# A list-scheduled hybrid decoder trunk: new transfer costs in its planner, one strip for the compressed bias, and its gates computed with Tanh

## The chip, the cores and the metric

The kernel runs on one core of a Trainium2 chip. Its time is the device time of one execution in microseconds (us), as the median of the runs. The core has a matmul engine (TensorE, PE; its weight loads are shown as PEld), three engines for elementwise work (VectorE, DVE; ScalarE, ACT; GpSimd, POOL) and SyncE, whose queue (SP) issues every transfer of this kernel. Each engine is given its own list of instructions, and waits by semaphore for what another engine or a transfer has to deliver.

## The reference

Two layers on 1024 tokens of width 1024, in float32. Each layer is `x + rms_post(W_out[(A | B | C) * silu(z)])` with `h = rms_pre(x)`, and one projection of `h` gives the columns of all groups and the gate path `z`.

- A (4 heads of 64): the sum of three attentions, each times a sigmoid gate per token and head. The first sees compressed keys: 63 overlapping blocks of 32 tokens pass a two-layer network, `silu(blk @ w1) @ w2`. The second sees all earlier tokens (16 of 16 blocks are selected), the third the last 512.
- B (4 heads): latent attention; queries and keys come out of normed low-rank latents, with a rotary part.
- C (8 heads): a window of 128 tokens, with a learned sink per head.

A and C add a relative-position bias from a table of 32 buckets per head. What the change touches is

```python
p_c = softmax(where(valid_c, lc + bias[:, t5_bucket(pos - cend)], NEG)) * valid_c
g = sigmoid(gates)
mixed = concat([o_a, o_b, o_c]) * silu(z)
```

## The kernel before

**Number format and tiles.** Each f32 operand is split into two f16 halves, and a product is three f16 matmuls (high-high, high-low, low-high), scaled by powers of two (`SW` = 256 on weights, `SQ` = 16 on activations, `SM` = 16 on the mixed output). `split` is one ACT copy, which writes the high half, and one DVE op, which writes the remainder. Tokens go in 8 tiles of 128. The kernel uses 8 banks of PSUM: three for scores (psS), two for transposes (psT), one for attention outputs (psO), two for projections (psJ).

**Stages of a layer.** `first` projects values, keys and the compressed blocks. `second` is a generator of further projections (latents, queries); `run` lays its pieces between the units of the sliding-window attention C. `gate_path` is the next generator: 26 tiles (3 column groups of 8 token tiles, and 2 tiles of the fourth) of 24 matmuls each give `z` in 128x256 blocks, laid between the units of attention A. Each block is copied out of PSUM by ACT (line 864), and each pair of blocks is stored to device memory (line 866). `last_phase` runs the latent attention B, the last 6 gate blocks, the product with `W_out` and the residual; in layer 1 the pre-norm of layer 2 as well.

**A unit** of attention is one token tile and one or two heads, in three parts that `run` keeps some units apart: `score` (matmuls into psS, then per piece one DVE op that scales, adds the bias strip, stores to SBUF and keeps the running minimum, then one Exp on ACT with the row sum), `turn` (transposes and splits the probabilities; by transposing DMA from a staging buffer in the larger units of attentions A and C and in the latent attention of layer 2 from its third token tile on, by PE otherwise) and `values` (matmuls into psO). In the latent attention the last of four units ends with `end_mla`: DVE multiplies the four heads out of psO into columns 256 to 511 of the gate tile.

**The gate in the last phase.** For each token tile `gate` (line 1176) fetches 128x1024 of `z` into a tile `sz` (two buffers), applies SiLU on ACT over the full width (line 1179), and POOL multiplies in the outputs of A and C. After `end_mla`, `mixed` (line 1184) splits the whole tile and transposes it by DMA for the product with `W_out`. The table that ACT needs for SiLU, sigmoid or Exp is loaded by an instruction of its own wherever the function changes to one that the loaded table lacks.

**The compressed bias.** It depends on the token and the block's end, so on 16 times the block index less the token: within a row group a shift by 8 columns per token tile. For each token tile `score` fetched it with 8 small transfers (lines 900 to 905) from `bias_rows` in device memory into a tile for four heads, with two buffers; column 63 was set to the masking value once a layer (line 1112).

**The order.** Nothing is emitted as it is written. Every instruction is recorded as a `Step`, with the steps it depends on and the buffers it uses. `schedule` (line 273) then simulates the engines: each free engine takes, of its steps whose inputs and buffers are ready, the one with the smallest key. The key is the number in program order, and for transfers the negative length of the longest chain behind the step. Buffers of a tag are handed out in program order. The prices are in `cost` (line 244): for a transfer the issue time on SP, its share of one common bus, and a fixed time to landing. The order that comes out is the order of every engine's instructions.

Of the kernel before, what the change touches and what calls it, by code (L numbers as in the profile page):

```python
# [15 lines left out]
F32 = mybir.dt.float32  # L16
# [9 lines left out]
SW = 256.0  # L26
# [13 lines left out]
L_M = 126  # L40
# [48 lines left out]
def row_mask():  # L89
    return (np.arange(128) >= 31).astype(np.float32).reshape(128, 1)  # L90

# [55 lines left out]

class Room:
# [17 lines left out]
class Step:  # L166


    def __init__(self, n, engine, name, args, kwargs):
        self.n, self.engine, self.name, self.args, self.kwargs = n, engine, name, args, kwargs  # L170
        self.before, self.after, self.rooms, self.key = set(), [], [], n


class Recorder:
# [9 lines left out]
    def __init__(self, nc):  # L184
        self.nc, self.steps, self.rooms, self.seen, self.inner = nc, [], [], {}, set()
        for name in ("tensor", "vector", "scalar", "gpsimd", "sync"):
            setattr(self, name, Recorder.Engine(self, name))
# [15 lines left out]
    def add(self, engine, op, args, kwargs):  # L203
        s = Step(len(self.steps), engine, op, args, kwargs)
# [39 lines left out]
    def cost(self, s):  # L244
# [13 lines left out]
        if s.engine == "vector":  # L258
            t = 152.0 + 1.045 * n
# [9 lines left out]
        if s.name == "dma_start_transpose":  # L269
            return 1300.0, (400.0 + size / 220.0, 2000.0)  # L270
        return 520.0, (size / 200.0, 1900.0)

    def schedule(self, slots):
# [13 lines left out]
        for s in reversed(self.steps):  # L287
# [3 lines left out]
            s.key = -tail[s] if s.engine == "sync" else s.n  # L291
        events, order, bus, table, now = [], [], [0.0], [None], 0.0
# [25 lines left out]
        while True:  # L318
            for e, heap in ready.items():
                if heap and free[e] <= now:  # L320
# [4 lines left out]
                    if e == "scalar" and s.args[2] not in (AF.Copy, AF.Square, table[0]):  # L325
                        table[0] = s.args[2]
                        busy, seen = busy + 1283.0, seen + 1283.0
                    if e == "sync":
                        bus[0] = max(bus[0], now + busy) + seen[0]
                        seen = bus[0] + seen[1] - now  # L330
                    s.seen = now + seen
# [32 lines left out]
def trunk(ctx, tc, a, out):  # L364
# [67 lines left out]

    rows_d = nc.dram_tensor("bias_rows", (12, L_ALL), F32, kind="Internal").ap()
# [62 lines left out]
    def bias_setup():  # L496
# [4 lines left out]
        for c0 in range(0, L_ALL, 1024):  # L501
# [9 lines left out]
            dma(rows_d[:, c0:c0 + n], rw[:, :n])  # L511
        for h in range(4):
# [129 lines left out]
    def compress_hidden(L, l, xs):  # L642
# [5 lines left out]
        for s in range(2):  # L648
# [8 lines left out]
            nc.scalar.activation(hid[:, s, :NC_CMP], p[:, :NC_CMP], AF.Silu, bias=hb[:, s:s + 1], scale=1.0 / (SW * SQ))  # L657

    def compressed(L):
# [7 lines left out]
        split(p[:, :64], SQ, L.KM[:, 0], L.KM[:, 1])  # L667
        for half in range(2):
            nc.tensor.matmul(p[64 * half:64 * half + 64, 128:192], hid[:, 1], w2[:, 128:], start=True, stop=True)
        for half in range(2):  # L670
            r = slice(64 * half, 64 * half + 64)
            split(p[r, 128:192], SQ, L.VM[r, half, 0], L.VM[r, half, 1])

    def first(L, l, wv):
# [27 lines left out]
        nc.scalar.activation(L.G, L.G, AF.Sigmoid, scale=1.0 / SW)  # L702
# [156 lines left out]
    def gate_columns(L, w, g, t, zs):  # L859
# [4 lines left out]
        nc.scalar.activation(zt[:, t % 2], p[:, :256], AF.Copy, scale=1.0 / SW)  # L864
# [16 lines left out]
    class Unit:  # L881
# [9 lines left out]
        def score(u):  # L891
# [7 lines left out]
            if kind == "cmp":  # L899
                if "cm" not in g["tile"]:  # L900
                    cm = g["tile"]["cm"] = view(L.r, 3072 + 256 * (qt % 2), [128, 4, 64], F32)
                    for i in range(8):
                        dma(cm[i * 16:(i + 1) * 16, :, :NC_CMP],
                            rows_ap(0, O_M + 63 - 8 * qt - i, [[L_M, 16], [L_ALL, 4], [1, NC_CMP]]))
                cm = g["tile"]["cm"]
                b = u.b = u.rings[0].take([128, 128], F32)
                p = ps("S")
                for j in range(2):
                    h = u.h + j
                    r = slice(j * 64, j * 64 + 64)  # L910
                    for s in range(2):
                        nc.tensor.matmul(p[:, r], L.QA[:, h, qs], L.KM[:, s], start=(s == 0), stop=(s == 1))
                    ttr(b[:, r], p[:, r], cm[:, h], ALPHA, BIGF, mx[:, 3 * j:3 * j + 1])
# [3 lines left out]
            if kind == "swa":  # L917
# [4 lines left out]
                for j in range(2):  # L922
# [3 lines left out]
                    for s in range(2):  # L926
                        nc.tensor.matmul(p[:, r], L.QC[:, h, qs], L.KC[:, s, k0 * 128:k0 * 128 + nk],
                                         start=(s == 0), stop=(s == 1))
                    ttr(b[:, r], p[:, r], L.stC[:, h, 256 - nk:], ALPHA, L.nsink[:, h:h + 1], mx[:, col:col + 1])
# [123 lines left out]
    def run(units, filler, total, lag_t, lag_v):  # L1053
# [5 lines left out]
        for i in range(n + lag_v):  # L1059
# [7 lines left out]
            while more and spent < total * done / whole:  # L1067
                w = next(filler, None)
                more = w is not None
                spent += w or 0  # L1070
        for _ in filler:
            pass

# [15 lines left out]
    def nsa_units(L):  # L1089
# [8 lines left out]
        for qt in range(NT):  # L1098
            tile = {}
# [245 lines left out]
```

## Time and profile before

| | us |
|---|---|
| median of 3 runs | 1091.31 (1089.62 to 1092.93) |
| profiled execution, its time | 1093.32 |
| profiled execution, span of its instructions | 1091.5 |
| PE busy / weight loads | 998.0 / 669.3 |
| DVE busy | 760.5 |
| ACT busy | 691.0 |
| POOL busy | 117.2 |

The mean granted PE clock is 0.968 of full speed. How to read it: a group line names the engine, the operation, what it writes and reads, shapes, the count, then busy time and the mean of one, then the idle time of the engine just before, with what ended it. Nearly all instructions bear line 359, where the planned order is emitted, so groups are told apart by their tiles. A stage begins and ends in the order of the plan, not at a barrier, so the windows by which the span is cut are cut by eye: the sliding-window stage of layer 1 from 115 to 233 us, attention A from 233 to 404, the latent stage from 404 to 558; in layer 2 from 640, 751 and 923.

### The profile page before, as it was taken

The page shows a single profiled execution, that of the slowest core. Times are in us where ns is not written, and L with a number is a line of the kernel's source. Part 1 is how long each engine was busy: PE and PEld are TensorE (multiplying, and loading weights), DVE is VectorE, ACT ScalarE, POOL GpSimd, SP SyncE. Part 2 cuts the span into 40 slices and gives each one's busy share as a digit, 9 for nine tenths or more (in the row PEclk, how much of TensorE's full clock was granted, in tenths as well). Part 3 has the DMA queues.
Part 4 walks back from the last instruction along what each step waited for, and adds up shares of the span by engine and source line. Part 5 has one row for each costly group of instructions (what it writes and reads, how often), then busy time and mean ns, then how long its engine had stood idle before and what let it go on. Part 6 is the DMA issues. An engine that isn't in the chain of part 4 may idle for free. (4 is left out here: it accounts for less than half of the span.)

```text
span 1091.5 us, 25293 instructions
## 1 busy us (share of the span) xinstructions
PE 998.0 (91%) x9536; PEld 669.3 (61%) x9536; DVE 760.5 (70%) x2268; ACT 691.0 (63%) x1655; POOL 117.2 (11%) x198
## 2 busy tenths in 40 slices
PE   5998999989999988999999999998999999599975
PEld 2853657648887774565575465764887777245432
DVE  4744678847788967878765367884778897677742
ACT  5642667737777867778545267773787787867731
POOL 1000101001110112212000010100111011212100
PEclk9999999989999998999999999998999999699988
DMA  7586467675499995775575546867448999676982
GB/s 254 147 268 174 91 151 143 135 159 138 96 153 190 190 249 149 177 159 135 114 190 184 136 102 141 150 132 160 131 104 149 187 192 236 141 172 151 212 174 77
DMA packets 313498, 174.41 MB, mean 160 GB/s; under 512 B 273580, under 2 KB 289324, under 8 KB 313376
## 3 DMA queue, kind: packets, MB, share of 16 engines
q1 hardware_dynamic: 313376, 172.81, 69.9%
q8 instruction: 74, 1.21, 0.5%
q14 instruction: 48, 0.39, 0.1%
HBM read 76.63 MB, written 21.41 MB: 90 GB/s over the span
## 5 line engine op out<-in xcount | busy, mean ns | idle before, releaser
L359 PEld LDWEIGHTS <-HT 128*128 128x128 f16 x3084 | 252.1, 99 | 44.0 <-issue 11.0
L359 ACT ACTIVATE arena<-arena,mx 128x256 f32<-128x256 f32 (+8 forms) x384 | 226.8, 591 | 82.4 <-DVE mx L359 80.7
L359 PE MATMUL psJ<-W,HT 128*128 128x256 f16 (+1 forms) x2304 | 270.9, 264 | 2.0 <-ACT sz L359 1.8
L359 PEld LDWEIGHTS <-arena 128*128 128x128 f16 x3540 | 169.2, 99 | 80.8 <-issue 11.1
L359 PE MATMUL psJ<-HT,W 128*128 128x512 f16 x864 | 199.9, 388 | 9.5 <-DVE tmp L359 6.2
L359 PEld LDWEIGHTS <-W 128*128 128x128 f16 x864 | 85.1, 100 | 109.5 <-issue 16.5
L359 PE MATMUL psO<-V,arena 128*128 128x64 f16 x2304 | 103.2, 193 | 6.7 <-DMA arena<-sz 5.3
L359 DVE CUSTOM_DVE_ANT_0 arena<-psS,R 128x64 f32<-128x64 f32 (+4 forms) x192 | 86.9, 464 | 31.0 <-PE psS L359 23.7
L359 ACT ACTIVATE sz<-psJ 128x256 f32<-128x256 f32 (+1 forms) x92 | 40.4, 440 | 83.0 <-PE psJ L359 55.9
L359 POOL TENSOR_TENSOR rs<-rs,halfneg 128x1 f32<-128x1 f32 x64 | 35.0, 548 | 529.1 <-DVE rs L359 513.5
L359 PE MATMUL psS<-KA,QA 128*128 128x512 f16 (+3 forms) x384 | 82.5, 313 | 0.1
L359 DVE CUSTOM_DVE_ANT_0 arena<-psS,arena,nsink 128x256 f32<-128x256 f32 (+1 forms) x128 | 57.6, 461 | 27.8 <-PE psS L359 27.5
L359 PE MATMUL psS<-KB,QB 96*128 96x512 f16 (+3 forms) x288 | 64.2, 346 | 12.3 <-DVE mx L359 11.9
L359 ACT ACTIVATION_READ_ACCUMULATOR arena<-arena,mx 128x1 f32 x384 | 72.7, 189 | 0.0
L359 ACT ACTIVATE arena<-psT 128x128 f16<-128x128 f32 (+3 forms) x144 | 53.9, 383 | 25.4 <-PE psT L359 20.6
L359 DVE SCALAR_TENSOR_TENSOR arena<-psT,arena 128x128 f16<-128x128 f32 (+3 forms) x144 | 60.3, 430 | 11.8 <-ACT arena L359 11.3
L359 PEld LDWEIGHTS <-V 128*128 128x128 f16 x384 | 36.6, 100 | 51.0 <-DMA V<-ringS 10.0
L359 PE MATMUL psT<-ident,arena 128*128 128x128 f32 x300 | 59.5, 290 | 7.1 <-DVE arena L359 3.9
L359 DVE SCALAR_TENSOR_TENSOR W<-ringS,W 128x1024 f16<-128x1024 f32 x48 | 58.4, 1223 | 10.5 <-ACT W L359 10.3
L359 DVE SCALAR_TENSOR_TENSOR sz<-arena,sz 128x512 f16<-128x512 f32 (+4 forms) x76 | 57.6, 758 | 11.1 <-ACT sz L359 11.1
L359 PE MATMUL psJ<-R,arena 128*128 128x65 f16 (+1 forms) x384 | 55.2, 300 | 2.4 <-DMA arena<-ringS 2.4
L359 ACT ACTIVATE psJ<-psJ 128x512 f32<-128x512 f32 x32 | 18.6, 582 | 59.4 <-DVE tmp L359 59.4
(132 smaller groups left out, 1548.4 us busy)
## 6 DMA issues: line engine op xcount, KB each, us to landing
ringS<-in_w_in_dram SPq DMA_DIRECT2D x40, 512.0 KB, 4.6
gate_rows<-sz SPq DMA_DIRECT2D x32, 256.0 KB, 3.2
ringS<-in_w_out_dram SPq DMA_DIRECT2D x16, 512.0 KB, 6.6
sz<-gate_rows SPq DMA_DIRECT2D x16, 512.0 KB, 4.5
R<-in_x_dram SPq DMA_DIRECT2D x8, 512.0 KB, 4.8
ringS<-in_cmp_w_dram SPq DMA_DIRECT2D x8, 512.0 KB, 5.9
x<-in_rope_dram SPq DMA_DIRECT2D x8, 512.0 KB, 4.8
x<-in_x_dram SPq DMA_DIRECT2D x8, 512.0 KB, 4.2
```

Of the source, the lines that this page charges most:

```text
L359: getattr(getattr(self.nc, s.engine), s.name)(*[real(v) for v in s.args], **{k: real(v) for k, v in s.kwargs.items()})
```

## The change

- **Planner.** Prices for transfers and for short DVE operations are new: issue 400, 485 or 650 ns by kind, bus at 300 rather than 200 bytes per ns, landing 1300 (transposes 1100) plus `SLACK` of 1200 ns. A transfer is issued in the plan only when the eighth last one has landed. Steps that `run` takes from a generator (the filler) get 60 added to their key. Exp and Tanh count as one table.
- **Order of recording.** In units of two heads (compressed and sliding window) the matmuls of both heads are recorded ahead of the first head's DVE and ACT steps.
- **Compressed bias.** A resident tile `mstrip` of 128 x 4 x 120 is filled by 8 transfers after the bias rows are stored; each token tile takes a window of 64 columns of it. The rows in device memory are one column longer, which holds the mask. The 64 small transfers and two memsets of each layer go.
- **Gates.** SiLU and sigmoid become Tanh: `silu(u) = u * (1 + tanh(u/2)) / 2`. For `z` the Tanh is taken where the block leaves PSUM, a DVE operation multiplies by the value in PSUM, and twice the SiLU is stored; the factor goes into the scale of `mixed`'s split. The full-width SiLU of the last phase goes. The hidden layer of the compressed blocks and the gates of A are turned likewise, with small DVE operations.

```diff
-L_M = 126
+L_M = 127
+W_M = 120
...
+
+
+LATE = 60
+
+
+
+SLACK = 1200.0
...
+TABLE = {AF.Exp: 0, AF.Tanh: 0, AF.Silu: 1, AF.Sigmoid: 2}
...
-        self.before, self.after, self.rooms, self.key = set(), [], [], n
+        self.before, self.after, self.rooms, self.key = set(), [], [], n + late
...
-            t = 152.0 + 1.045 * n
+            t = max(152.0 + 1.045 * n, 250.0)
...
         if s.name == "dma_start_transpose":
-            return 1300.0, (400.0 + size / 220.0, 2000.0)
-        return 520.0, (size / 200.0, 1900.0)
+            return 900.0 + size / 600.0, (size / 300.0, 1100.0 + SLACK)
+        inner = isinstance(out, View) and isinstance(src, View)
+        return 400.0 if size > 500000 else 650.0 if inner else 485.0, (100.0 + size / 300.0, 1300.0 + SLACK)
...
-            s.key = -tail[s] if s.engine == "sync" else s.n
-        events, order, bus, table, now = [], [], [0.0], [None], 0.0
+            if s.engine == "sync":
+                s.key = -tail[s]
+        events, order, bus, table, lanes, now = [], [], [0.0], [None], [], 0.0
...
-                if heap and free[e] <= now:
+                if heap and free[e] <= now and (e != "sync" or len(lanes) < 8 or lanes[-8] <= now):
...
-                    if e == "scalar" and s.args[2] not in (AF.Copy, AF.Square, table[0]):
-                        table[0] = s.args[2]
+                    if e == "scalar" and TABLE.get(s.args[2], table[0]) != table[0]:
+                        table[0] = TABLE[s.args[2]]
                         busy, seen = busy + 1283.0, seen + 1283.0
...
+                        lanes.append(now + seen)
...
+        for i in range(8):
+            dma(mstrip[i * 16:(i + 1) * 16], rows_ap(0, O_M + 7 - i, [[L_M, 16], [L_ALL, 4], [1, W_M]]))
...
-            nc.scalar.activation(hid[:, s, :NC_CMP], p[:, :NC_CMP], AF.Silu, bias=hb[:, s:s + 1], scale=1.0 / (SW * SQ))
+            hv = sb([128, 2, 64], F32, "hv", 2)
+            nc.vector.tensor_scalar(hv[:, 0, :NC_CMP], p[:, :NC_CMP], 1.0 / (SW * SQ), hb[:, s:s + 1], op0=OP.mult, op1=OP.add)
+            nc.scalar.activation(hv[:, 1, :NC_CMP], hv[:, 0, :NC_CMP], AF.Tanh, scale=0.5)
+            nc.vector.scalar_tensor_tensor(hid[:, s, :NC_CMP], hv[:, 1, :NC_CMP], 1.0, hv[:, 0, :NC_CMP],
+                                           op0=OP.add, op1=OP.mult)
...
-        split(p[:, :64], SQ, L.KM[:, 0], L.KM[:, 1])
+        split(p[:, :64], SQ / 2, L.KM[:, 0], L.KM[:, 1])
...
-            split(p[r, 128:192], SQ, L.VM[r, half, 0], L.VM[r, half, 1])
+            split(p[r, 128:192], SQ / 2, L.VM[r, half, 0], L.VM[r, half, 1])
...
-        nc.scalar.activation(L.G, L.G, AF.Sigmoid, scale=1.0 / SW)
+        nc.scalar.activation(L.G, L.G, AF.Tanh, scale=0.5 / SW)
+        nc.vector.tensor_scalar(L.G, L.G, 0.5, 0.5, op0=OP.mult, op1=OP.add)
...
-        nc.scalar.activation(zt[:, t % 2], p[:, :256], AF.Copy, scale=1.0 / SW)
+        nc.scalar.activation(zt[:, t % 2], p[:, :256], AF.Tanh, scale=0.5 / SW)
+        nc.vector.scalar_tensor_tensor(zt[:, t % 2], zt[:, t % 2], 1.0, p[:, :256], op0=OP.add, op1=OP.mult)
...
             if kind == "cmp":
-                if "cm" not in g["tile"]:
-                    cm = g["tile"]["cm"] = view(L.r, 3072 + 256 * (qt % 2), [128, 4, 64], F32)
-                    for i in range(8):
-                        dma(cm[i * 16:(i + 1) * 16, :, :NC_CMP],
-                            rows_ap(0, O_M + 63 - 8 * qt - i, [[L_M, 16], [L_ALL, 4], [1, NC_CMP]]))
-                cm = g["tile"]["cm"]
+                cm = mstrip[:, :, 56 - 8 * qt:120 - 8 * qt]
...
                     for s in range(2):
                         nc.tensor.matmul(p[:, r], L.QA[:, h, qs], L.KM[:, s], start=(s == 0), stop=(s == 1))
+                for j in range(2):
+                    h = u.h + j
+                    r = slice(j * 64, j * 64 + 64)
                     ttr(b[:, r], p[:, r], cm[:, h], ALPHA, BIGF, mx[:, 3 * j:3 * j + 1])
                     expo(b[:, r], mx[:, 3 * j:3 * j + 1], sm[:, 3 * j:3 * j + 1])
...
                         nc.tensor.matmul(p[:, r], L.QC[:, h, qs], L.KC[:, s, k0 * 128:k0 * 128 + nk],
                                          start=(s == 0), stop=(s == 1))
+                for j in range(2):
+                    h = u.h + j
+                    col = h % 4
+                    r = slice(j * nk, j * nk + nk)
                     ttr(b[:, r], p[:, r], L.stC[:, h, 256 - nk:], ALPHA, L.nsink[:, h:h + 1], mx[:, col:col + 1])
                     expo(b[:, r], mx[:, col:col + 1], sm[:, col:col + 1])
...
             while more and spent < total * done / whole:
+                nc.late = LATE
                 w = next(filler, None)
+                nc.late = 0
                 more = w is not None
                 spent += w or 0
+        nc.late = LATE
         for _ in filler:
             pass
+        nc.late = 0
...
-        for i in range(2):
-            nc.vector.memset(view(L.r, 3072 + 256 * i, [128, 4, 64], F32)[:, :, 63:], MASKED)
...
         def gate(qt):
             sz = tiles[qt]["sz"] = sb([128, D], F32, "sz", 2)
             dma(sz, z_d[qt * 128:(qt + 1) * 128, :])
-            nc.scalar.activation(sz, sz, AF.Silu)
...
             hl = nxt["hl", 0]
-            split(g["sz"], SM, hl[:, 0], hl[:, 1])
+            split(g["sz"], SM / (2 * SW), hl[:, 0], hl[:, 1])
```

More of the change, by code (lines that the diff above doesn't have):

```diff
@@ L166, with __init__ @@
 class Step:
-    def __init__(self, n, engine, name, args, kwargs):
+    def __init__(self, n, late, engine, name, args, kwargs):
         self.n, self.engine, self.name, self.args, self.kwargs = n, engine, name, args, kwargs
-        self.before, self.after, self.rooms, self.key = set(), [], [], n
+        self.before, self.after, self.rooms, self.key = set(), [], [], n + late
 class Recorder:
@@ L185, in __init__ @@
         self.nc, self.steps, self.rooms, self.seen, self.inner = nc, [], [], {}, set()
+        self.late = 0
         for name in ("tensor", "vector", "scalar", "gpsimd", "sync"):
@@ L203, in add @@
     def add(self, engine, op, args, kwargs):
-        s = Step(len(self.steps), engine, op, args, kwargs)
+        s = Step(len(self.steps), self.late, engine, op, args, kwargs)
         self.steps.append(s)
@@ L431, in trunk @@
     nc.vector.memset(zero, 0.0)
+    mstrip = sb([128, 4, W_M], F32, "mstrip")
     rows_d = nc.dram_tensor("bias_rows", (12, L_ALL), F32, kind="Internal").ap()
@@ L1098, in nsa_units @@
         for qt in range(NT):
-            tile = {}
             for h in (0, 2):
-                g = {"tile": tile}
+                g = {}
                 r.append(Unit(L, "cmp", qt, h, g, None, rings))
```

## The prediction

> **What bounds the kernel now.** I read the page's busy shares first, then the span cut by stage, then who TensorE (PE) waited for, and last the timeline of the worst stretch.
>
> ```profile
> PE 998.0 (91%) x9536; PEld 669.3 (61%) x9536; DVE 760.5 (70%) x2268; ACT 691.0 (63%) x1655; POOL 117.2 (11%) x198
> ```
>
> PE is busy for 91% of the span, so no edit to another engine is worth more than the 93 us in which PE stands still, plus what PE loses while its granted clock is low. The stage table says where these are. Its columns are the window and its length, the busy time (and instructions) of each engine, the granted PE clock, the DMA share and GB/s.
>
> ```profile
> 0.00:26.00 26.00, 12.87 (x32) 5.46 (x33) 11.19 (x22) 12.79 (x21) 2.90 (x10) 1.00 0.73 260
> 26.00:115.00 89.00, 84.67 (x589) 51.03 (x589) 45.69 (x85) 37.91 (x71) 2.19 (x4) 0.98 0.64 183
> ...
> 233.00:404.00 171.00, 166.87 (x2053) 133.47 (x2053) 131.12 (x445) 124.27 (x331) 22.25 (x45) 0.98 0.80 162
> 404.00:558.00 154.00, 142.49 (x1099) 80.88 (x1095) 115.45 (x297) 106.39 (x188) 25.22 (x33) 0.94 0.64 158
> ...
> 751.00:923.00 172.00, 166.58 (x2057) 133.92 (x2056) 131.53 (x444) 123.85 (x333) 22.24 (x45) 0.98 0.80 159
> 923.00:958.00 35.00, 22.33 (x137) 10.95 (x138) 22.39 (x73) 26.69 (x45) 6.90 (x9) 0.71 0.64 174
> 958.00:1042.00 84.00, 80.25 (x628) 41.28 (x627) 61.72 (x167) 57.61 (x89) 15.28 (x15) 1.00 0.80 179
> 1042.00:1091.50 49.50, 29.92 (x196) 14.08 (x193) 14.94 (x22) 8.45 (x16) 1.64 (x3) 0.84 0.53 123
> ```
>
> The sparse attention stages (233 to 404, 751 to 923) leave PE only 4.1 and 5.4 us idle. The weak places are the latent attention stage of layer 1 (11.5 us idle, clock 0.94), the first 35 us of the same stage in layer 2 (12.7 us idle, clock 0.71) and the last 49.5 us (19.6 us idle, clock 0.84). The start idles 13.1 us before any of the changed work. In 923 to 958 PE waited for these, as total, times, longest:
>
> ```profile
> PE psS L359 <- DVE mx L359: 6.4, 3, 3.8
> PE psO L359 <- DVE sz L359: 3.9, 2, 3.0
> ```
>
> The timeline of ACT, DVE, SyncE's queue (SP) and PE shows what stands behind the 3.0 us: start, length, instruction.
>
> ```profile
> 940.04 1.04 ACT L359 ACTIVATE W<-ringS 128x1024 f16<-128x1024 f32 x1
> 941.09 1.28 ACT L359 ACT_TABLE_LOAD   x1
> 942.39 1.06 ACT L359 ACTIVATE sz<-sz 128x1024 f32<-128x1024 f32 x1
> ...
> 944.29 1.28 ACT L359 ACT_TABLE_LOAD   x1
> ...
> 943.48 0.86 DVE L359 SCALAR_TENSOR_TENSOR sz<-psO,rc,sz 128x64 f32<-128x64 f32 x4 [1.14 <-ACT sz L359]
> ...
> 936.62 0.33 SPq L359 DMA_DIRECT2D sz<-gate_rows  x1
> ...
> 944.39 1.12 PE L359 MATMUL psO<-VB,HT 128*128 128x64 f16 x18 [3.00 <-DVE sz L359]
> 947.64 0.58 PE L359 MATMUL psS<-KB,QB 96*128 96x512 f16 x1 [2.13 <-DVE mx L359]
> ```
>
> The gate tile is fetched at 936.62. ACT then loads a table (1.28) and applies SiLU (1.06); only now may DVE multiply the attention output by it, and only then is PE's one output bank free.
>
> **The change, part by part.** These groups give the prices: busy us, mean ns.
>
> ```profile
> L359 ACT ACT_TABLE_LOAD x35 | 44.9, 1283 | 3.0 <-DVE mx L359 1.7 <-PEq L1335 0.7
> L359 ACT ACTIVATE sz<-sz 128x1024 f32<-128x1024 f32 x16 | 16.9, 1056 | 0.9 <-DMA sz<-gate_rows 0.8
> L359 ACT ACTIVATE sz<-psJ 128x256 f32<-128x256 f32 x64 | 23.8, 374 | 29.4 <-PE psJ L359 18.8 <-DMA gate_rows<-sz 6.1 <-issue 2.9
> L359 DVE SCALAR_TENSOR_TENSOR W<-ringS,W 128x1024 f16<-128x1024 f32 x48 | 58.4, 1223 | 10.5 <-ACT W L359 10.3
> L359 DVE TENSOR_TENSOR QC<-psO,rc 128x256 f32<-128x256 f32 x32 | 13.4, 420 | 3.7 <-PE psO L359 2.9 <-DVE mx L359 0.2
> L359 ACT ACTIVATE arena<-arena,mx 128x256 f32<-128x256 f32 x136 | 68.4, 503 | 29.7 <-DVE mx L359 29.1
> ```
>
> *Tanh for SiLU and sigmoid.* If Tanh is served by the table that Exp uses, 34 of the 35 loads go: 34 x 1.283 = 43.6 us of ACT. The 16 full-width SiLUs go too: 16.9 us. All 16 and 28 of the loads lie in the latent stages, so ACT loses 52.8 us of its work there. The 64 copies of gate columns become 64 Tanh; no row has a Tanh, so it is bounded by the copy (0.374) and by an Exp of that width (0.503). I take the copy, since it too reads PSUM and has no bias or sum: no change, at worst 64 x 0.13 = 8.3 us of ACT.
>
> What of it reaches PE? Not the whole: in 958 to 1042 ACT made ten loads and five SiLUs, and PE was still busy 80.25 of 84 us. I count where PE stands. In 923 to 958 the waits on sz (3.9) go. The 2.13 us wait that ends at 947.64 and the 3.8 us one before it have a share of ACT's queue in them; the splits of the output weights keep their 1.2 us each on DVE, so I take half of 6.4, 3.2. The clock of 0.71 over 35 us is 10.2 us of lost cycles, of which half, 5, returns when the gaps that precede it go. Together 12. In 404 to 558 the clock lost 0.06 x 154 = 9.2 and idle is 11.5; less of it names the gate:
>
> ```profile
> PE psT L359 <- DVE arena L359: 2.4, 3, 1.4
> PE psS L359 <- DVE mx L359: 2.3, 3, 0.8
> PE psO L359 <- DVE sz L359: 0.5, 1, 0.5
> ```
>
> I take half of 2.4 + 2.3 + 0.5 and 3.4 of clock, 6. In the last 49.5 us one wait on sz goes, the 1.8 that the 3.9 and 0.5 leave of the 6.2 in the whole span (its row stands with the schedule, below): 2. **Sum -20.** The bounds: 0 (ACT never set PE's pace) and -45 (12.7 + 10.2 + 11.5 + 9.2 and 1.8, all idle and clock loss of the two stretches).
>
> The Trainium skill, ScalarE: Activation LUTs, "What ACT_TABLE_LOAD costs", prices a switch at 1283 ns of load plus a drain of about 1380 ns. The load agrees with the row to the nanosecond. The drain does not show: at 941.09 the load starts 0.01 us after the split before it. By the page ACT would be freed of 34 x 2.66 = 90 us, an estimate; the sum goes by the row.
>
> *The gate product on DVE.* Each of the 64 gate tiles gets a 128x256 scalar_tensor_tensor out of PSUM. The nearest row is 0.420 with f32 out of PSUM: 26.9 us of DVE, of which 26 tiles per layer, 10.9 us, lie in the sparse stage, where DVE then has 142 of 171 us. The projection bank (psJ, two of them) is now given back after ACT and DVE, not after ACT. PE works behind it on attention and on the other bank, which is the cover; without it every tile costs 0.42. Bounds 0 and +26.9; near the first, because that stage's PE has under 6 us idle and DVE 29 us free: **+3.** On SP, the store of the gate pair waits for that product too, and what is queued behind it is transposes.
>
> *Small ones.* Four hidden tiles get one tensor_scalar and one scalar_tensor_tensor of 63 columns, the gates one tensor_scalar per layer; four memsets go. At the 0.42 us of the 256-column row as a ceiling the ten are 4.2 us of DVE, in stages where it is half idle (45.69 of 89 us busy from 26 to 115): 0, bounds 0 and +4.2.
>
> *The bias strip.* One resident strip replaces 128 small transfers:
>
> ```profile
> L359 SPq DMA_DIRECT2D R<-bias_rows x128: 302/424/1766, 229.9 to 864.1; - x128
> ...
>   DVE arena L359: 3.1, 2
> ```
>
> (min/median/max ns on the queue; who waited for the landing, us, times.) SP is freed of 128 x 0.424 = 54 us of issue, and DVE of waits of 3.1 us. Eight issues of the same kind, 3.4 us, come into the bias setup behind the four row stores and ahead of the twelve replicating transfers. Bounds -3.1 and +3.4; the replicated rows are first read in the next stage, and DVE has slack where it waited: **-1.**
>
> *The schedule.* The planner's prices, the late fillers and two heads' scores issued ahead of their evictions change the order on every engine. By its own formula a 512 KB load was planned at 520 + 2621 + 1900 = 5.0 us and is now 400 + 100 + 1748 + 2500 = 4.7; a 128 KB copy inside SBUF goes from 3.1 to 3.7; a transpose of 128x1024 f16 from 4.9 to 4.5. Measured landings:
>
> ```profile
> ringS<-in_w_in_dram SPq DMA_DIRECT2D x40, 512.0 KB, 4.6
> ...
> QC<-sz SPq DMA_DIRECT2D x16, 128.0 KB, 3.0
> ...
> arena<-sz SPq DMA_TRANSPOSE x76, 3.7
> ```
>
> The plan was not far off before, so I expect a small gain from waits on landings. PE's waits on those are the prize, and the two stage borders the risk:
>
> ```profile
> PE psJ L359 <- DMA V<-ringS: 8.9, 3, 5.0
> PE psJ L359 <- DVE tmp L359: 6.2, 2, 3.2
> PE psO L359 <- DVE sz L359: 6.2, 4, 3.0
> PE psO L359 <- DMA arena<-sz: 5.3, 5, 1.9
> PE psO L359 <- DMA HT<-HT: 3.4, 1, 3.4
> PE psJ L359 <- DMA arena<-ringS: 2.4, 2, 2.1
> ```
>
> The DMA rows sum to 20.0 us. I take a quarter, **-5**; bounds -20 and, since a new order can as well create such waits, +13 (the 6.2 us of waits on DVE tmp at the borders and the clock loss of those stages, 2 x 0.02 x 171 = 6.8, once more).
>
> The sum is -20 + 3 + 0 - 1 - 5 = -23. The profiled execution took 1093.3 us (span 1091.5 and 1.8 around it), 2.0 above the median of 1091.3; against itself it goes to 1070.3, and the median to **1068**.
>
> **The rivals.** *DVE and the banks become the bound (slower).* Evidence for: DVE is at 77% in the sparse stages and would be at 83%, with W splits of 1.2 us in its queue ahead of a product that holds a bank. Against: two banks, and 24 matmuls per tile between two uses. It decides if a bank is held longer than PE has other work ready. Then all 26.9 us count, half of the 20 is eaten as the last gate tiles drain into the latent stage, and order gives 3: 1091.3 + 26.9 - 10 - 3 = 1105.
>
> *ACT's relief does not reach PE.* For: the 958 to 1042 row. Against: the 941 chain. Then the first term is 3, and 1091.3 - 3 + 3 - 1 - 2 = 1088.
>
> *The stalls and the low clock go entirely.* For: a low clock follows the gaps, so both go together. Against: the W splits at the stage's start. 12.7 + 10.2 of layer 2, 14 of layer 1's stage (two thirds of 11.5 + 9.2) and 10 (half of the waits on landings): 1091.3 - 47 = 1044.
>
> *Late fillers pile up at the stage ends.* Fillers now yield by 60 steps, so more projection is left when the attention units are out. The border shows the price of projections alone:
>
> ```profile
> 233.41 1.01 PE L359 MATMUL psJ<-HT,W 128*128 128x512 f16 x2 [3.16 <-DVE tmp L359]
> ```
>
> 3.2 us and 3.4 of clock (0.02 x 171), in each layer: as much again is +13, so 1068 + 13 = 1081.
>
> *The loads stay.* Were Tanh not in Exp's table, every gate tile in the sparse stage would cost two loads: 52 x 2.57 = 133 us of ACT, 124 + 67 = 191 us in a stage of 171, some 20 us over in each layer: above 1130. No row has a Tanh to decide it. The Trainium skill, ScalarE: Activation LUTs, "Table sets: the hidden batching unit", lists tanh in the set whose anchor is exp; by that page this rival does not occur, which is why its chance is small.
>
> **How the numbers follow.** Forecast 0.43, entire removal 0.20, late fillers 0.12, bound by DVE 0.12, no reach 0.10, loads stay 0.03. About 0.3% (3.3 us) is what a measurement here can tell from no change. Faster: 0.43 + 0.20 + 0.10 of the late fillers + 0.04 of no reach = 0.77; the same: 0.06 + 0.02 = 0.08; slower: 0.12 + 0.03 = 0.15. The range takes in the forecast, no reach, late fillers, half of entire removal and the lower part of the DVE case: 1042 to 1098, some 0.8.
>
> **What would show it.** One table load in the whole trace (the loads rival falls or stands with that). No SiLU group of width 1024; 64 Tanh of about 0.37 to 0.50 us; 64 more products of 0.42 us on DVE. In the latent stage of layer 2 the wait of psO on DVE sz is gone and the clock of its first 35 us is above 0.85. In the sparse stages PE stays within 8 us of the stage length; if waits of psJ on DVE sz there exceed 10 us, the DVE rival is at work. Waits of psJ on DVE tmp above 10 us speak for late fillers. I am wrong if the gain lies mainly in the sparse or sliding-window stages, or if the first 35 us of the layer 2 stage stay at a clock of 0.7 with the loads gone.

## The result, and the profile after

The changed kernel takes 1054.51 us (median of 4 runs, 1053.57 to 1056.28) against 1092.12 us for the kernel before in the same comparison: a ratio of 0.9659, 95% interval 0.9634 to 0.9683, or 37.6 us less. The forecast was 1068, with a range of 1042 to 1098. The time lies in the range, 14 us under the forecast. The profiled execution took 1054.55 us (span 1052.8, mean granted PE clock 0.981 against 0.968). First the busy shares of the changed kernel:

```profile
PE 987.3 (94%) x9536; PEld 664.8 (63%) x9536; DVE 774.7 (74%) x2338; ACT 633.0 (60%) x1605; POOL 126.9 (12%) x198
```

PE executes the same 9536 matmuls. Its busy time fell by 10.7 us, which goes with the higher clock, and its idle time from 93.5 to 65.5 us, by 28.0; together that is the 38.7 us by which the span is shorter. ACT lost 58.0 us and DVE gained 14.2.

For the comparison by stage I cut every span at the first matmul of each stage on PE. These cuts are not the prediction's, which were made by eye, and they move when projections move across a border. Microseconds, both layers together where one number stands:

| | before | after | change |
|---|---|---|---|
| start and `first` | 188.4 | 188.3 | -0.1 |
| sliding window | 224.1 | 221.0 | -3.1 |
| sparse attention | 318.6 | 308.6 | -10.0 |
| latent, layer 1 | 172.9 | 168.9 | -4.0 |
| latent, layer 2, to the end | 187.5 | 166.0 | -21.5 |

Windows of the changed kernel, in the columns of the prediction's stage table: the head, the sparse stages, the latent stage of layer 1, then the first 35 us of that of layer 2, the 35 us that follow, and the last 49.5 us of the span.

```profile
26.60:113.40 86.80, 84.72 (x576) 49.37 (x575) 47.38 (x89) 34.65 (x66) 3.35 (x4) 1.00 0.66 189
223.70:378.70 155.00, 148.94 (x1824) 118.50 (x1823) 125.60 (x439) 112.28 (x303) 22.18 (x42) 0.98 0.75 151
378.70:547.60 168.90, 157.59 (x1332) 94.09 (x1330) 131.16 (x337) 96.80 (x196) 30.23 (x36) 0.97 0.69 169
733.20:886.80 153.60, 148.85 (x1824) 118.81 (x1823) 125.67 (x437) 112.31 (x303) 22.16 (x42) 0.98 0.74 151
886.80:921.80 35.00, 27.51 (x324) 20.25 (x322) 29.62 (x94) 24.43 (x57) 8.45 (x10) 0.94 0.99 233
922.00:957.00 35.00, 34.56 (x236) 17.04 (x235) 24.82 (x66) 15.84 (x34) 8.20 (x8) 0.96 0.82 177
1003.30:1052.80 49.50, 36.27 (x253) 17.78 (x251) 18.40 (x35) 10.62 (x20) 3.82 (x5) 0.91 0.62 133
```

The weakest 35 us of the layer 2 stage, ahead of its end, had 12.7 us idle at a clock of 0.71. Now the weakest are the first 35, with 7.5 us idle at 0.94, and in the next 35 PE idles 0.4 us. (Counted like these from the stage's first matmul, at 904.00, the first 35 us of the kernel before had 8.7 us idle at 0.90; its weak stretch came later.) The last 49.5 us went from 19.6 us idle at 0.84 to 13.2 at 0.91. The groups that the change touches:

```profile
L375 ACT ACT_TABLE_LOAD x1 | 1.3, 1283 | 0.7 <-PEq L1362 0.7
L375 ACT ACTIVATE sz<-psJ 128x256 f32<-128x256 f32 x64 | 23.9, 373 | 5.2 <-PE psJ L375 4.6
L375 DVE SCALAR_TENSOR_TENSOR sz<-sz,psJ 128x256 f32<-128x256 f32 x64 | 26.6, 415 | 0.0
```

One table load is left of 35. A Tanh costs 373 ns, what the copy cost, and the product 415 ns. PE's waits over the whole span, as total, times, longest:

```profile
PE psS L375 <- DVE mx L375: 12.5, 17, 3.7
...
PE psJ L375 <- DVE tmp L375: 6.7, 2, 3.7
...
PE psO L375 <- DVE sz L375: 1.1, 1, 1.1
...
PE psJ L375 <- DVE sz L375: 0.7, 4, 0.2
```

All rows of PE's waits on landings sum to 13.8 us (before: 21.6), those on DVE to 40.5 (54.8), those on ACT to 2.0 (8.3). The wait of psO on the gate tile fell from 6.2 to 1.1, and the new product makes PE wait 0.7 us in all. For the end, PE's waits in the last 49.5 us, first of the changed kernel, then of the kernel before:

```profile
PE psO L375 <- DMA HT<-HT: 4.5, 2, 3.5
PE psO L375 <- DVE sz L375: 1.1, 1, 1.1
PE psJ L375 <- DMA arena<-ringS: 0.2, 1, 0.2
```

```profile
PE psJ L359 <- DMA V<-ringS: 5.0, 1, 5.0
PE psO L359 <- DMA HT<-HT: 3.4, 1, 3.4
PE psJ L359 <- DMA arena<-ringS: 2.1, 1, 2.1
PE psO L359 <- DVE sz L359: 1.8, 1, 1.8
```

Of 12.3 us of waits at the end 5.8 remain, and nearly all that went were landings of weights and activations, not the gate.

### The profile page after: what moved, and what is told of

Its sections match the earlier page's. It is cut to its first block, busy times and chain, and to the rows that moved or that the text cites. A ratio compares the mean times of both kernels' runs of the same rounds, so it can differ in the third digit from the quotient of the medians.

```text
span 1052.8 us, 25180 instructions
## 1 busy us (share of the span) xinstructions
PE 987.3 (94%) x9536; PEld 664.8 (63%) x9536; DVE 774.7 (74%) x2338; ACT 633.0 (60%) x1605; POOL 126.9 (12%) x198
## 4 chain that ended last, share of the span: by engine, by line
PE 72%; DMA 11%; DVE 9%; issue 4%; ACT 2%; SPq 0%; POOL 0%; POOLq 0%; DVEq 0%; ACTq 0%
PE psJ L375 51%; PE psS L375 10%; PE psO L375 7%; PE psT L375 4%; DVE arena L375 3%; DMA arena<-sz 2%; DMA arena<-stage_win 1%; DVE sz L375 1%; DMA arena<-stage_slc 1%; DMA arena<-ringS 1%; DMA arena<-KC 1%; DVE W L375 1%; DMA x<-in_rope_dram 1%; DMA arena<-in_norm_pre_dram 1%; DVE tmp L375 1%
## 5 line engine op out<-in xcount | busy, mean ns | idle before, releaser
L375 PE MATMUL psJ<-W,HT 128*128 128x256 f16 (+1 forms) x2304 | 283.0, 264 | 0.0
L375 PEld LDWEIGHTS <-arena 128*128 128x128 f16 x3540 | 179.4, 98 | 76.8 <-issue 6.4
L375 PE MATMUL psJ<-HT,W 128*128 128x512 f16 x864 | 202.9, 387 | 7.7 <-DVE tmp L375 6.7
L375 PE MATMUL psO<-V,arena 128*128 128x64 f16 x2304 | 132.4, 193 | 5.3 <-DMA arena<-stage_slc 2.3
L375 DVE CUSTOM_DVE_ANT_0 arena<-psS,R 128x512 f32<-128x512 f32 (+3 forms) x128 | 74.1, 585 | 17.2 <-PE psS L375 16.7
L375 PE MATMUL psS<-KA,QA 128*128 128x512 f16 (+3 forms) x384 | 85.8, 313 | 0.7 <-DVE mx L375 0.7
L375 DVE SCALAR_TENSOR_TENSOR arena<-psT,arena 128x128 f16<-128x128 f32 (+3 forms) x144 | 59.9, 429 | 13.4 <-ACT arena L375 12.4
L375 DVE CUSTOM_DVE_ANT_0 arena<-psS,arena,nsink 128x256 f32<-128x256 f32 (+1 forms) x128 | 56.2, 460 | 17.7 <-PE psS L375 17.7
L375 POOL TENSOR_TENSOR tmp<-tmp 128x128 f32<-128x128 f32 x32 | 19.6, 612 | 314.2 <-DVE tmp L375 295.2
```

What stands on the lines that cost most here:

```text
L375: getattr(getattr(self.nc, s.engine), s.name)(*[real(v) for v in s.args], **{k: real(v) for k, v in s.kwargs.items()})
```

## The experiments

The theory at this point: the table loads and the full-width SiLU were what held the latent stages, and the new order adds a little. The rival: the order is the main thing. In the table, "to before" and "to after" are the differences of the medians, in us (the kernel before ran again beside each group of runs, with medians of 1091.32 to 1092.48; the changed kernel is that of the result); the stage columns are the spans of the profiled execution, cut as above, both layers together (before 318.6 and 360.4, after 308.6 and 334.9).

| run | median | ratio, 95% interval | to before | to after | sparse | latent |
|---|---|---|---|---|---|---|
| Tanh alone | 1085.71 | 0.9947, 0.9921 to 0.9972 | -5.6 | +31.2 | 318.8 | 351.3 |
| strip alone | 1103.51 | 1.0101, 1.0051 to 1.0150 | +12.2 | +49.0 | 327.6 | 360.3 |
| planner and order alone | 1085.07 | 0.9933, 0.9906 to 0.9961 | -6.3 | +30.6 | 321.6 | 346.3 |
| all but Tanh | 1067.53 | 0.9775, 0.9726 to 0.9823 | -23.8 | +13.0 | 308.6 | 340.2 |
| after, SiLU put back unplanned | 1079.80 | 0.9869, 0.9825 to 0.9912 | -12.2 | +25.3 | 308.2 | 359.0 |
| after, product twice | 1074.40 | 0.9827, 0.9790 to 0.9864 | -17.6 | +19.9 | 323.8 | 339.7 |
| Tanh and strip | 1092.67 | 1.0002, 0.9985 to 1.0020 | +0.7 | +38.2 | 325.7 | 351.2 |
| after, no limit of eight | 1049.48 | 0.9604, 0.9566 to 0.9643 | -42.5 | -5.0 | 310.0 | 334.2 |
| after, late fillers off | 1063.06 | 0.9754, 0.9715 to 0.9793 | -29.4 | +8.6 | 312.7 | 338.1 |
| after, slack 0 | 1072.23 | 0.9829, 0.9787 to 0.9870 | -20.3 | +17.7 | 318.0 | 337.6 |
| after, old transfer prices | 1091.41 | 0.9999, 0.9976 to 1.0022 | -1.1 | +36.9 | 312.4 | 354.6 |
| after, old order of scores | 1081.43 | 0.9913, 0.9890 to 0.9937 | -11.1 | +26.9 | 319.9 | 333.8 |

### Tanh alone

The hunks that turn SiLU and sigmoid into Tanh, on the kernel before, and the two lines of the planner that count Exp and Tanh as one table:

```diff
+TABLE = {AF.Exp: 0, AF.Tanh: 0, AF.Silu: 1, AF.Sigmoid: 2}
...
-        nc.scalar.activation(zt[:, t % 2], p[:, :256], AF.Copy, scale=1.0 / SW)
+        nc.scalar.activation(zt[:, t % 2], p[:, :256], AF.Tanh, scale=0.5 / SW)
+        nc.vector.scalar_tensor_tensor(zt[:, t % 2], zt[:, t % 2], 1.0, p[:, :256], op0=OP.add, op1=OP.mult)
...
-            nc.scalar.activation(sz, sz, AF.Silu)
```

> Only the gates are turned to Tanh (and the planner told that Exp and Tanh share a table); planner prices, fillers, recording order and bias transfers as before. Theory A (the table loads and the full-width SiLU held the latent stages back): 20 to 25 us off 1092, all of it after the first latent score of each layer, one table load left. Theory B (most of the 37.6 us is the new order): under 10 us off.

The loads fell to one and ACT lost as much as in the changed kernel (632.8 us busy), but the time fell by 5.6 us only. The latent stage of layer 2 shrank by 13.9 us, that of layer 1 grew by 4.8, and the start by 3.2. ACT's relief is not what the 37.6 us are made of. The weak stretch of the layer 2 stage stays, without a single load in it; its window, and PE's longest wait there:

```profile
918.00:953.00 35.00, 24.88 (x249) 17.14 (x248) 28.00 (x94) 21.65 (x54) 8.41 (x10) 0.80 0.92 217
```

```profile
PE psS L362 <- DVE mx L362: 9.7, 4, 6.0
```

PE idles 10.1 us at a clock of 0.80, where it was 12.7 at 0.71. The waits of psO on the gate tile are gone from this stretch, but the wait of psS on DVE mx, of which I had put half down to ACT's queue, went from 6.4 to 9.7 us. Over the whole span PE's waits for the gate tile are these, first with Tanh alone, then in the run below that has the planner alone and every SiLU in place:

```profile
PE psO L362 <- DVE sz L362: 4.6, 2, 4.3
```

```profile
PE psO L374 <- DVE sz L374: 0.9, 1, 0.9
```

With Tanh alone the waits of layer 2 are gone, but one of 4.3 us in layer 1 is new, and no SiLU stands on its chain: the tile's fetch is issued at 418.73 us, DVE has two splits of output weights before its product at 423.65, and PE goes on at 424.55. With the planner alone hardly a wait is left. So the order decides these waits at least as much as the SiLU does.

### The strip alone

```diff
-                if "cm" not in g["tile"]:
...
+                cm = mstrip[:, :, 56 - 8 * qt:120 - 8 * qt]
```

> Only the bias strip. Theory A: 0 to 3 us off 1092, since SyncE does not set the end. Theory C (54 us of issue freed on SyncE is what shortened the sparse stages): 8 to 12 us off, in the sparse stages.

128 small transfers fewer, and the kernel is 12.2 us slower, 9.0 of it in the sparse stages from which they were taken. SP was freed there as foreseen (its issues take 84 and 85 us of the two stages against 120 and 118), and the time still rose. Neither expectation had a loss. With this work taken away, only the order that the old plan made of the rest is left to blame; that is an inference. It is not the transfer prices alone: the changed kernel with the old prices, further below, has the strip too and its sparse stages take 312.4 us.

### The planner and the order of scores alone, and all but Tanh

The first is the changed kernel with Tanh and strip undone; the second has Tanh undone only.

> Only the planner (transfer prices, slack, eight in flight, late fillers, short DVE prices) and the order of recording; SiLU, sigmoid and the 128 small transfers as before. Theory A: 5 to 12 us off 1092. Theory B: 25 us off or more.

> The whole change without Tanh: planner and strip, with SiLU and sigmoid as before. Theory A: 1075 to 1082, so 20 to 27 us above the changed kernel, 35 table loads. Theory B: 1060 to 1067. If the parts add, this is the sum of the runs with the strip alone and the planner alone.

Two parts that bring -6.3 and +12.2 apart bring -23.8 together. The second kernel still makes its table loads and SiLUs, with 39 loads against 35:

```profile
L375 ACT ACT_TABLE_LOAD x39 | 50.0, 1283 | 1.4 <-PEq L1357 0.7
L375 ACT ACTIVATE sz<-sz 128x1024 f32<-128x1024 f32 x16 | 16.9, 1057 | 0.2
```

With all of them its latent stages take 340.2 us, 20.2 less than before. This contradicts the theory: the gain that I had put down to the loads comes without their removal. Tanh on top brings another 5.3 us there, and 13.0 in all. By the expectations the planner alone came out as theory A had it and Tanh alone as theory B; the run without Tanh, at 1067.53, lies just above the range of B (1060 to 1067) and well under that of A, and 30 us under the sum of its two parts.

Where the strip helps the new plan can be seen on SP's queue (start, length) in the sparse stage, first without the strip, then with it:

```profile
317.95 1.58 SPq L374 DMA_TRANSPOSE arena<-KC  x1
319.59 0.66 SPq L374 DMA_DIRECT2D R<-bias_rows  x1
320.30 0.42 SPq L374 DMA_DIRECT2D gate_rows<-sz  x1
320.83 1.35 SPq L374 DMA_TRANSPOSE arena<-stage_slc  x1
322.22 0.78 SPq L374 DMA_DIRECT2D gate_rows<-sz  x1
323.04 0.48 SPq L374 DMA_DIRECT2D ringS<-in_w_out_dram  x1
```

```profile
316.96 1.33 SPq L375 DMA_TRANSPOSE arena<-stage_slc  x1
319.04 1.32 SPq L375 DMA_TRANSPOSE arena<-stage_win  x1
323.56 1.44 SPq L375 DMA_TRANSPOSE arena<-sz  x1
```

Without the strip the queue has hardly a gap, so that a transpose is issued when its turn comes; with it the issues leave room (88 and 86 us of the two stages rather than 112 and 110). The sparse stages take 308.6 us with it and 321.6 without. That the tight queue is the cause is an inference from these rows, and a free queue is not enough: with the strip and the old order of scores SP's issues take as little (84 us each), and the sparse stages 319.9.

### Tanh and strip, without the planner

> Tanh and the strip on the planner of before. If the parts add, -5.6 + 12.2: 1098. If each new content only needs a plan whose transfer prices are right, the strip stays a loss here too (1095 to 1105). If the strip frees SyncE and its loss alone was an accident of one order: 1070 to 1085.

+0.7, with an interval around no change: what the two removals save on ACT and SP, 59 and 54 us of their queues, is worth nothing under the old plan. None of the three ranges expected had this time.

### SiLU put back without telling the planner

To price loads and SiLU at a fixed order, the changed kernel applies one SiLU to each gate tile where it stood, and the planner prices that step at nothing (each gate tile then passes one SiLU more than the reference has):

```diff
             dma(sz, z_d[qt * 128:(qt + 1) * 128, :])
+            nc.unplanned = True
+            nc.scalar.activation(sz, sz, AF.Silu)
+            nc.unplanned = False
```

> The changed kernel, with a full-width SiLU put back on the gate tile in the last phase, which the planner prices at zero, so that the order stays that of the changed kernel in all but a few dozen instructions. It applies SiLU to values that are gated already, so the output is not the reference's. This is the price of table loads and SiLU with the order held. Theory A (ACT's relief carries the gain): 20 us or more above the changed kernel, 1075 or more. Theory B (in the new order ACT has room): less than 8 us above, under 1063.

The order is nearly that of the changed kernel (about 110 of PE's 9536 matmuls stand elsewhere), and the time is 25.3 us above it: 24.1 us in the latent stages. ACT has 54.3 us more to do. Its timeline, and PE's, show one instance:

```profile
909.94 0.38 ACT L378 ACTIVATE sz<-psJ 128x256 f32<-128x256 f32 x1 [0.89 <-PE psJ L378]
910.34 1.28 ACT L378 ACT_TABLE_LOAD   x1
...
911.63 1.06 ACT L378 ACTIVATE sz<-sz 128x1024 f32<-128x1024 f32 x1
912.70 1.28 ACT L378 ACT_TABLE_LOAD   x1
914.00 0.40 ACT L378 ACTIVATE arena<-arena,mx 128x128 f32<-128x128 f32 x1
...
914.55 0.48 PE L378 MATMUL psT<-ident,arena 128*128 128x128 f32 x1 [3.77 <-ACT arena L378]
```

Two loads and a SiLU, 3.6 us, lie ahead of one Exp, and PE stands for 3.77 us. So the mechanism that I predicted exists, at 0.47 us of time per us of ACT (25.3 of 54.3). The run with all but Tanh has 67 us of such work, planned with its price, and pays 13.0 us for it. That a planner which knows the price puts these steps where they do little harm is the likely reason; no run shows it apart from the rest of the order.

### The product twice

```diff
+        nc.unplanned = True
+        nc.vector.scalar_tensor_tensor(spare, zt[:, t % 2], 1.0, p[:, :256], op0=OP.add, op1=OP.mult)
+        nc.unplanned = False
         nc.vector.scalar_tensor_tensor(zt[:, t % 2], zt[:, t % 2], 1.0, p[:, :256], op0=OP.add, op1=OP.mult)
```

> The changed kernel with the DVE product of each gate tile made twice, the first into a spare tile, priced at zero by the planner. 64 x 0.42 = 27 us more of DVE, and psJ held longer. Theory A (PE covers it): 0 to 4 us above 1054.5, with the waits of psJ still near nothing. Rival (DVE and the banks bind): 15 to 27 us above.

Another 26.5 us of DVE, which holds the bank a second time, costs 19.9 us, of which 15.2 lie in the sparse stages, as the rival expected and not theory A. The window of that stage in layer 1 (DVE is the third engine), and two rows of PE's waits in it:

```profile
221.30:383.30 162.00, 151.95 (x1824) 118.58 (x1823) 135.59 (x465) 113.19 (x303) 19.82 (x42) 0.98 0.72 144
```

```profile
PE psS L378 <- DVE mx L378: 3.1, 10, 0.7
...
PE psJ L378 <- DVE sz L378: 0.4, 1, 0.4
```

DVE goes from 125.6 us of 155.0 to 135.6 of 162.0, PE's idle time from 6.1 to 10.1. It is DVE's queue that PE waits for, not the bank: the wait on mx went from 0.4 to 3.1 us, in ten short pieces, and psJ waits 0.4 us for the product. The one product that the change adds cost nothing that shows, since the sparse stages took 308.6 us without it (all but Tanh) and with it. The cover is used up by the next one, at least where the planner does not know of it; about 430 of PE's matmuls stand elsewhere than in the changed kernel, so part of the loss may be order.

### One part of the planner at a time

From the changed kernel: the limit of eight transfers in flight taken out, `LATE = 0`, `SLACK = 0.0`, the old three transfer prices, and the matmuls of both heads no longer recorded first.

```diff
-                if heap and free[e] <= now and (e != "sync" or len(lanes) < 8 or lanes[-8] <= now):
+                if heap and free[e] <= now:
```

```diff
-            return 900.0 + size / 600.0, (size / 300.0, 1100.0 + SLACK)
+            return 1300.0, (400.0 + size / 220.0, 2000.0)
...
-        return 400.0 if size > 500000 else 650.0 if inner else 485.0, (100.0 + size / 300.0, 1300.0 + SLACK)
+        return 520.0, (size / 200.0, 1900.0)
```

> The changed kernel, whose planner does not hold a transfer back for the eighth last one. The order differs in a handful of instructions, so: within 3 us of 1054.5 if the model of eight in flight is not what brought the gain; 1060 or more if those few places matter.

> The changed kernel with fillers not set back (0 for 60). If the fillers' place is what shortened the sliding-window and latent stages: 1062 to 1075. If late fillers cost at the stage ends, as one rival had it: 1045 to 1050. Theory D (each order is one draw, no single knob carries the gain): within 5 us of 1054.5.

> The changed kernel with no slack for landings (0 for 1200 ns), so that a 512 KB load is planned at 3.5 us where 4.6 was measured. If slack is what keeps PE from waits on landings: 1065 to 1080, with PE's waits on transfers at 20 us or more against 13 in the changed kernel. Theory D: within 5 us of 1054.5.

> The changed kernel with the transfer prices of before (issue, bus, landing; no slack), eight in flight kept. By their own formulas old and new plan a 512 KB load at 5.0 and 4.7 us. If prices matter as little as the prediction had it: within 5 us of 1054.5. If the issue times and the bus are what the old plan had wrong: 1065 to 1080.

> The changed kernel with the old recording order in units of two heads (matmuls of a head, its DVE step, its Exp, then the next head). If the new order is what shortened the sliding-window stages: 7 us longer in these two together, 1060 or more. Otherwise within 4 us of 1054.5.

The old prices alone undo the whole change (ratio 0.9999), a larger loss than either expectation had. With them the other new parts of the planner bring nothing: 1091.41 us, against 1092.67 with Tanh and strip on the whole old planner. Against the changed kernel, the loss in that run is spread over nearly every stage: 9.1 us in the start and `first`, 4.2 in the sliding window, 3.8 in the sparse stages and 19.7 in the latent ones. One place shows what such an order looks like. In the head the rotary table `x` is issued behind seven strip transfers, DVE waits for it, and PE for DVE; the timeline of SP, DVE and PE:

```profile
91.01 2.77 SPq L374 DMA_DIRECT2D mstrip<-bias_rows  x6
...
97.74 0.43 SPq L374 DMA_DIRECT2D mstrip<-bias_rows  x1
98.22 0.42 SPq L374 DMA_DIRECT2D x<-in_rope_dram  x1
103.58 1.42 DVE L374 TENSOR_TENSOR tmp<-psJ,x 32x512 f32<-32x512 f32 x2 [6.26 <-DMA x<-in_rope_dram]
105.05 1.44 PE L374 MATMUL psJ<-HT,W 128*128 128x512 f16 x3 [3.86 <-DVE tmp L374]
```

In the changed kernel the last strip transfer is issued at 75.29 us and `x` at 89.20, and PE waits 0.4 us in all from 60 to 125. Which of the three prices moves them is not shown.

What slack does shows in PE's waits on landings, 40.2 us in all without it against 13.8 with it. The two largest rows without it:

```profile
PE psO L375 <- DMA arena<-sz: 11.3, 10, 2.3
PE psJ L375 <- DMA V<-ringS: 8.4, 5, 2.7
```

A landing that is planned 1.2 us early is one for which PE stands, in many short waits: 26.4 us more of them, for 17.7 us of time (its waits on DVE fell by 6.5).

So slack came out as expected. The late fillers are worth 8.6 us, not a loss. The order of the scores is worth 26.9 us, more than expected, with 12.4 of its loss in the sliding window (7 were expected) and 11.3 in the sparse stages. The limit of eight is worth less than nothing: without it the kernel takes 1049.48 us. That beats the kernel before; against the changed kernel the two intervals overlap (0.9566 to 0.9643, 0.9634 to 0.9683), so the 5.0 us are likely but not settled. Neither expectation had a gain. PE's list is the same from 48 us on, those of DVE and ACT from 100, and SP's but for one transfer in each sparse stage. In the head the profiles differ by just this time. The window of that kernel that answers to the first one above:

```profile
25.90:107.70 81.80, 80.95 (x579) 48.80 (x578) 47.39 (x90) 35.47 (x68) 3.80 (x4) 1.00 0.72 201
```

It is 5.0 us shorter: PE is busy 3.77 us less with the same matmuls, and idles 1.23 us less. What makes the same matmuls shorter stands in the last section.

## Why the prediction was right, and where it was wrong

The time was in the range and the sign was right. The chain of reasons was half wrong, and that the sum came so near is in good part luck: the term for Tanh was too large for what Tanh brings, and the term for the schedule far too small.

*The prices of the operations held.* One load, a Tanh that costs what the copy cost, 415 ns for the product, the wait of psO on DVE sz nearly gone (though by the order, as the next paragraph has it), a clock of 0.94 where 0.85 was the mark (a weak sign, since the kernel before has 0.90 when the stage is cut at its first matmul). The rival in which the loads stay fell with the first row.

*Tanh, -20: the step "What of it reaches PE" failed.* The latent stages did shrink, by 25.5 us, but 20.2 of that came with 39 loads still in place. I read the waits on the gate, half of those beside it and half of the lost clock as the price of the loads. With the loads gone on the old plan the waits on the gate went from 6.2 to 4.6 us, the wait of psS on DVE mx grew, and the clock of the weak stretch came back to 0.80 only. With the planner alone and the loads in place the waits on the gate were down to 0.9. So the order decided them in the main. Measured, Tanh is worth 5.6 us on the old plan, 13.0 on the new one, and 25.3 where the order is held. Only the last is what the step had worked out, and it is not what taking the loads out of a planned kernel brings.

*The end, -2: too small, because I counted one wait on the gate alone.* The last 49.5 us lost 6.4 us of idle time, and the landing waits there fell from 10.5 us to 4.7; the clock lost 3.5 us less ((0.91 - 0.84) x 49.5). The rows for it were in the profile, under landings, where I took a quarter of the total.

*The schedule, -5: the step "The plan was not far off before, so I expect a small gain" failed.* I compared the two formulas with the median landings, three kinds of transfer, and found them alike. But the old prices under the new rest give 1091.4. PE's waits on landings fell by 7.8 us, near the term, but not by the planner: with the planner alone they rose to 24.4 us, and with Tanh and strip on the old plan they fell to 12.6. What the planner lowered are waits that name DVE: 54.8 us before, 46.8 with the planner alone, 42.2 with the strip as well, but 59.6 with Tanh alone. A wait that names an engine can be a matter of order too, and I had counted only those that name a transfer.

*The product, +3, bounds 0 and 26.9:* 0 by the sparse stages, and the cover that I named is there: a second product costs most of its duration. The rival in which DVE becomes the bound fell for the change, at 0.7 us of waits. With a second product it comes true in part (19.9 of 26.5 us), by DVE's queue and not by the banks.

*The strip, -1: wrong by its context.* It is +12.2 on the old plan and, by the difference of two runs without Tanh, -17.5 on the new. I priced it by its own instructions, which stay right; what they are worth is set by the plan.

*Late fillers:* the waits of psJ on DVE tmp went from 6.2 to 6.7 us, and without the fillers' lateness the kernel is slower. This rival fell. *ACT's relief does not reach PE* came true for Tanh on the old plan, but its 1088 for the whole change did not. *The stalls and the low clock go entirely*, at 1044, was 10 us off on the other side; the forecast was off by 14.

What stays open: which of the three transfer prices (issue, bus, landing) matters; what the strip is worth in the changed kernel, since no run takes out the strip alone; and how far each single loss is the loss of that part or the mark of any other order, which no run tells apart. Each single reversal but one was slower, by 9 to 37 us, and the strip alone shows that a new order can cost 12 us where work was only taken away. Terms of this size do not add: alone the three parts come to -5.6 + 12.2 - 6.3 = +0.3, together to -37.6.

## What to carry to other kernels

Where the order is planned from prices, a removed instruction is worth what the plan makes of it: price it at a fixed order by adding it back unplanned, and with the plan by removing it, and expect two answers. Check the planner's landing times against the trace with a margin on the late side before cutting work, since here one set of transfer prices put back cost as much as the whole change brings. Parts of such a change are judged together, because an edit that only frees a queue can make the next order worse.

## What the runs showed of the hardware

*PE ran at about half its pace at the start although the clock column reads 1.00.* The head of the changed kernel and that of the kernel without the limit of eight have the same transposes and the same small products of the bias table. A window of the changed kernel's head, then rows of PE's timeline, the changed kernel first:

```profile
26.60:40.00 13.40, 13.40 (x61) 7.05 (x60) 9.00 (x13) 8.93 (x16) 1.81 (x3) 1.00 0.50 144
```

```profile
27.06 3.58 PE L375 MATMUL psS<-arena,relT 33*12 33x512 f32 x4
...
30.58 1.97 PE L375 MATMUL psT<-ident,x 128*128 128x128 f32 x8
...
41.13 1.03 PE L375 MATMUL psT<-ident,x 128*128 128x128 f32 x8
```

```profile
28.07 1.88 PE L375 MATMUL psS<-arena,relT 33*12 33x512 f32 x4
...
30.52 1.04 PE L375 MATMUL psT<-ident,x 128*128 128x128 f32 x8
```

Eight transposes take 1.97 us at 30.58 and 1.03 at 41.13 in one kernel, and 1.04 at 30.52 in the other; four bias products take 3.58 and 1.88. The trace's records of the granted clock begin at 37.0 us in the changed kernel and at 28.0 in the other; before its first record the column prints 1.00. Nine us more at half the pace account in size for the 3.77 us of busy time that the changed kernel loses. Until 34.3 us the changed kernel's order holds bias products (33 by 12 of the array) and transposes, and only two projection matmuls; the other order alternates them with projections. That the kind of work decides is a guess; no run held the rest alike.

The Trainium skill, TensorE: Matmul & The Clock Gate, Part 1 (The HAM clock gate), says that after a start PE has half its clock for a budget of about 3.4 us of time, not for a number of matmuls. Half the pace agrees with the rows; the 3.4 us do not, since PE is busy without a gap from 26.6 us and is still slow at 30.58.
